# An encoder layer with expert retrieval on one core: a norm's vector moved to the copies, later loads, shares of background work by stage, one value block in three split

## The chip, the cores and the metric

The kernel runs on 1 core of one Trainium2 chip. The time is the device time of one execution in microseconds (us). TensorE (PE) multiplies, with its weight loads (PEld) beside; VectorE (DVE), ScalarE (ACT) and GpSimd (POOL) work on elements; SyncE (SP) issues transfers, as ACT and POOL also do.

## The reference

Two batches of 256 tokens each (prompt and sample), preceded by 16 learned meta tokens, pass one layer of width 1024:

```python
def layer(h, tables, norm_mix_g, w_in, conv_w, ...):
    xn = rmsnorm(h, norm_mix_g)
    z = xn @ w_in
    gate_b, gate_c, hc, q, k, v = jnp.split(z, IN_SPLITS, axis=-1)
    y_conv = group_rmsnorm(gate_b * depthwise_conv3(gate_c * hc, conv_w), conv_out_g, CONV_GROUPS)
    ...
    y_attn = group_rmsnorm(gqa_attention(q, k, v), attn_out_g, N_HEADS)
    h = h + jnp.concatenate([y_conv, y_attn], axis=-1) @ w_out
    h = h + peer_ffn(rmsnorm(h, norm_ffn_g), peer_wq, peer_subkeys, peer_u, peer_v)
    return h

def peer_ffn(x, wq, subkeys, u_tab, v_tab):
    q = (xf @ wq).reshape(T, PEER_HEADS, 2, PEER_HALF)
    s = jnp.einsum('thpc,hpnc->thpn', q, subkeys)
    sv, si = lax.top_k(s, PEER_TOPK)
    ...
    cv, cp = lax.top_k(cand, PEER_TOPK)
    eidx = jnp.take_along_axis(cand_idx, cp, axis=-1)
    gates = jax.nn.softmax(cv, axis=-1)
    uc = jnp.take(u_tab, eidx, axis=0)
    a = jax.nn.gelu(jnp.einsum('thkd,td->thk', uc, xf), approximate=False) * gates
    vc = jnp.take(v_tab, eidx, axis=0)
    return jnp.einsum('thk,thkd->td', a, vc)
```

cand are the 16 x 16 sums of the best scores of two halves, so each token chooses 8 heads x 16 of 16384 experts. All numbers are fp32.

## The kernel before

The experts of the two batches are computed in two ways. For the prompt the rows of the chosen experts are **gathered**: one indirect transfer (grow, 1 MB) brings u and v of one expert for each of 128 tokens; DVE makes a dot product of u and x (a "dot"), ACT the gelu and the gate (dots), DVE adds the weighted v to the output row (xh, a "value"). There are 256 such gathers, in a ring of four buffers. For the sample all 16384 experts are computed **densely**: 128 blocks of u against all tokens (pSj), a dense matrix of gates made on the chip (pgm), and 128 blocks of v against the weighted result A (acc).

PE's stages, in the order of the program:

- *First front end* (s=0, to 135 us): norm, transposes (`norm_T`), input projection, convolution, attention, output projection. Each product is split into three fp32r terms (high and low parts: whi, wlo, xT, lo).
- *First projections* (to 189 us): queries, key scores (`key_scores`), top-k of token tile 0 on DVE.
- *Second front end* (s=1, to 341 us): the same with plain fp32 matmuls. Beside it runs background work: the gathers, and the top-k of tile 1 as a task.
- *Second projections* (to 415 us), with key scores put off by `lag=3`.
- *U stage* (to 924 us): the loop over 128 blocks of u (128x1024, 512 KB each). `experts` applies the gelu to four blocks at a time (SG). The task `gates_dense` ends the top-k (`fin1`), transposes idx_i and idx_j (pi) and the gates (pg), makes one-hot masks oi and oj on DVE and their scaled copies gh and gl on ACT, and multiplies them on PE (pgm), four tokens a step; each pair of steps is then multiplied into A (Al and Ah, blocks 0 to 91 and 92 to 127).
- *Values stage* (to 1345 us): `values(j)` for 128 blocks of v, loaded in pairs. A block is direct (eight fp32 matmuls of 128x512) or, one in SPL, split: ACT makes ah and vh (vhl), DVE al and vl, and PE twelve fp32r matmuls. vhl has one pair of buffers.

The order of the background work is set when the program is written. `bg(us)` follows each piece of PE work and gives credits: `share["a"]` of the microseconds to gathers (each costs GU=2.65), `share["b"]` to tasks, whose `yield` numbers say what a step costs. `gather()` then emits a dot, a value and the next issues. In the values stage the gathers that are left are spread evenly over the blocks. Each engine works through its instructions in that order; POOL issues a gather when a ring buffer is free, and not before the matmul that stood last on PE when it was emitted (`sync_dep`).

SP's queue carries the loads of x, weights, u and v; ACT's queue a few others: gf (the second norm's vector, broadcast to 512 KB) at the start and dc0 (192 KB, constants for decoding the top-k) at the first projections. xg is the first norm's vector, broadcast to 512 KB and used in the norm:

```python
dve.scalar_tensor_tensor(x, h[:, t, :], stat, xg, op0=ALU.mult, op1=ALU.mult)          # 494
act.activation(dst(cs), pt, AF.Copy)                                                   # 466
dve.tensor_tensor(dst_lo(cs), pt, dst(cs).bitcast(F32), op=ALU.subtract)               # 468
```

Of the kernel before, what the change touches and what calls it, by code (L numbers as in the profile page):

```python
# [8 lines left out]
F32 = mybir.dt.float32  # L9
# [3 lines left out]
AF = mybir.ActivationFunctionType  # L13
ALU = mybir.AluOpType
# [4 lines left out]
P = 128  # L19
D = 1024  # L20
NC = 8
NT = 4
SEQ = 256
NM = 16
# [12 lines left out]
JH = 92  # L37
SF = 0.5
SB0 = 0.35
SR = 0.6  # L40
SS = 0.72
SMAX = 0.74
SPL = 4
SBS = 0.42
# [3 lines left out]
def encoder_layer(ctx: ExitStack, tc: tile.TileContext, xp, xs_, meta, vec, w_in, w_out, wq,  # L48
                  skT, qkg, gffn, gmixr, rope, iota16, dec, u_t, uv, v_n, yp, ys):
    nc = tc.nc  # L50
# [326 lines left out]
    def projections(xr, sk, scores, qp, step=None, split=False, rescale=None, lag=1):  # L377
# [3 lines left out]

        def key_scores(hp, qs):
            pn = pst.tile([P, 2, P], F32, tag="tr", name="pn")
            for t in range(2):
                pe.matmul(pn[:, t, :], qs[:, t * P:(t + 1) * P], sk[:, hp, :], start=True, stop=True)
            if hp < 2 and rn is not None:
                for t in range(2):
                    act.activation(scores[:, hp, t], pn[:, t], AF.Copy, scale=rn[:, t:t + 1])
            else:
                act.activation(scores[:, hp], pn, AF.Copy)  # L390
            if step is not None and hp % 2:
                step(hp // 2)

        for hd in range(PH):
            w = weights(wq, hd, split)
            for pp in range(2):
# [9 lines left out]
                bg(3.9)  # L406
        while late:
            key_scores(*late.pop(0))

# [19 lines left out]
    nc.sync.dma_start(vecs, vec)  # L429
    xg = one.tile([P, D], F32, name="xg")  # L430
    nc.sync.dma_start(xg, bass.AP(tensor=gmixr.tensor, offset=gmixr.offset, ap=[[0, P], [1, D]]))
    w_kv = weights(w_in, 0, True)
# [7 lines left out]
    gf = one.tile([P, D], F32, name="gf")  # L440
    act.dma_start(gf, bass.AP(tensor=gffn.tensor, offset=gffn.offset, ap=[[0, P], [1, D]]))

# [16 lines left out]
    def norm_T(dst, x, dst_lo=None):  # L459
        for c4 in range(2):  # L460
            pt = (pst, pss)[c4].tile([P, 4, P], F32, tag=("tr", "sc")[c4], name="pt")
            for cc in range(4):
                c = 4 * c4 + cc
                pe.transpose(pt[:, cc, :], x[:, c * P:(c + 1) * P], ident)
            cs = slice(4 * c4, 4 * c4 + 4)
            act.activation(dst(cs), pt, AF.Copy)
            if dst_lo is not None:
                dve.tensor_tensor(dst_lo(cs), pt, dst(cs).bitcast(F32), op=ALU.subtract)

    def front(s, h, rn):  # L470
# [17 lines left out]
        for t in range(2):  # L488
# [4 lines left out]
            x = tmp.tile([P, D], F32, tag="xs", name="xs")  # L493
            dve.scalar_tensor_tensor(x, h[:, t, :], stat, xg, op0=ALU.mult, op1=ALU.mult)
            tok = slice(NM + t * P, NM + (t + 1) * P)
            norm_T(lambda c: xT[:, c, tok], x, (lambda c: xTl[:, c, tok]) if sp else None)
            bg(1.2)
        if s == 0:
# [3 lines left out]
            rsqrt(mstat[:, 1:2], mstat[:, 0:1], 1, 1.0 / D)  # L502
            dve.scalar_tensor_tensor(mt, mt, mstat[:, 1:2], xg[:NM], op0=ALU.mult, op1=ALU.mult)
            pm = pst.tile([P, NC, NM], F32, tag="tr", name="pm")
            for c in range(NC):
                pe.transpose(pm[:, c, :], mt[:, c * P:(c + 1) * P], ident[:NM, :NM])
            act.activation(xTm, pm, AF.Copy)
        dve.tensor_copy(xT[:, :, 0:NM], xTm)
# [24 lines left out]
        def k_T(a, rows, dst):  # L533
# [5 lines left out]
            act.activation(dst, pk[:, :, :rows], AF.Copy)  # L539

        w = w_kv if s == 0 else weights(w_in, 0)
        for t in (0, 1, -1) if s == 0 else (0, 1):
# [142 lines left out]
        def conv_fin(i, cstat):  # L685
# [9 lines left out]
            if sp:  # L695
                act.activation(catT[:, i, :], yn, AF.Copy)
                dve.tensor_tensor(catTl[:, i, :], yn, catT[:, i, :].bitcast(F32), op=ALU.subtract)

        st = {}
        cs_ = None  # L700
# [23 lines left out]
        def turn(sl):  # L724
# [6 lines left out]
            for c in range(2):  # L731
                k = 2 * sl + c
                act.activation(xr[:, k], pt[:, c], AF.Copy, scale=vecs[:, 8 + k:9 + k])
                if sp:
                    dve.scalar_tensor_tensor(xrl[k // 4][:, k % 4], pt[:, c], vecs[:, 8 + k:9 + k], xr[:, k].bitcast(F32),
                                             op0=ALU.mult, op1=ALU.subtract)

        for sl in range(4):
            w = weights(w_out, sl, sp)
# [42 lines left out]
    dc0 = r0p.tile([P, 3, 16, 16], F16, name="dc0")  # L782
    act.dma_start(dc0, dec)
    sc0 = r0p.tile([P, NC * (LK + 256)], F32, tag="sc", name="sc0")[:, :32 * P].rearrange("p (h t n) -> p h t n", h=16, t=2)
# [26 lines left out]
    queue.extend((0, k) for k in range(P))  # L811
    share.update(a=SF, b=SB0)
    rn1 = selp.tile([P, 2], F32, name="rn1")
# [59 lines left out]
    share.update(a=SR, b=0.0)  # L873
    projections(xr1, sk1, sc1, q1, step1, rescale=rescale, lag=3)
    direct[0] = True
# [7 lines left out]
    def gates_dense():  # L883
# [4 lines left out]
        topk_left[0] = -1  # L888
        yield 10.0
        ogx = ExitStack()  # L890
# [34 lines left out]
        for t in range(2):  # L925
# [12 lines left out]
            for r in range(2):  # L938
                act.activation(dup[:, 0:2, :, r], pi, AF.Copy)
            yield 1.6  # L940
            for o in range(P // OC):
                s0 = o * OC
# [12 lines left out]
                if len(steps) > 1:  # L955
                    gate_products(*steps.pop(0))
                yield 1.3 + (4 * r_done[0] + 60) / 700
        gate_products(*steps.pop(0))
        ogx.close()

    tasks.append(gates_dense())
    share.update(a=SS, b=SBS)
    late = []
# [14 lines left out]
    for j in range(P):  # L978
# [8 lines left out]
        if j % SG == 0 and j:  # L987
            experts(*late.pop(0))
        bg(3.5)
    experts(*late.pop(0))  # L990
# [57 lines left out]
def layout(**inputs):  # L1048
# [15 lines left out]
    def wl(a):  # L1064
# [26 lines left out]
        skT=c(g("peer_subkeys")[0].reshape(16, P, P).transpose(2, 0, 1)),  # L1091
        qkg=qkg, gffn=g("norm_ffn_g"), gmixr=g("norm_mix_g"), rope=rope, iota16=iota, dec=dec,
        u_t=c(u.reshape(P, P, NC, P).transpose(3, 1, 2, 0).reshape(P, P, D)), uv=c(np.concatenate([u, v], axis=1)), v_n=v)
# [19 lines left out]
```

## Time and profile before

| | |
|---|---|
| median of 3 runs | 1352.38 us (1351.4 to 1353.75) |
| profiled execution | 1352.28 us, span 1350.5 us, mean granted clock 0.984 |
| PE busy | 1275.4 us, 94% of the span |
| PEld, DVE, ACT, POOL busy | 957.6, 1043.2, 536.2, 387.4 us |
| bytes moved | 460.19 MB, 341 GB/s over the span |
| chain that ended last | PE 51%, transfers 10%, DVE 8% of the span |

Busy shares are means over stages with different limits. The windows view gives them by stage, the list of waits says what ended PE's idle time, and the timeline shows single instructions with their start and length. A row names the engine, the line, the operation, the tile written and the tiles read.

### The profile page before, as it was taken

The numbers are of one execution on the slowest core, as the hardware profiler recorded it, in microseconds if no ns is written. First come the engines' busy times: TensorE is split into PE (matmuls) and PEld (weight loads), VectorE is DVE, ScalarE is ACT, GpSimd is POOL, SyncE is SP. The second block draws the span as 40 slices with busy tenths as digits, with TensorE's granted clock in tenths as the row PEclk, the third lists the DMA queues.
The fourth block names the chain that finished last, engine by engine and source line by source line (L and its number), as shares of the span: only waits on it lengthen the run. The fifth ranks groups of instructions, "written<-read, shape, count | busy, mean of one in ns | idle before, by whom it ended". The sixth has DMA issues, their size and how long they took to land.

```text
span 1350.5 us, 17724 instructions
## 1 busy us (share of the span) xinstructions
PE 1275.4 (94%) x5998; PEld 957.6 (71%) x5998; DVE 1043.2 (77%) x2247; ACT 536.2 (40%) x1576; POOL 387.4 (29%) x480
## 2 busy tenths in 40 slices
PE   5999998888898999779999999998999999999998
PEld 5888996667787887668788888885555555555554
DVE  5656998976699998688887978986767667676665
ACT  4555531752221311176776766641222222222121
POOL 1111124432242334434332322332222223223121
PEclk9999998998998999979999999999999999999999
DMA  5434646576998999999999999999999999999997
GB/s 204 131 103 159 205 123 228 203 267 255 374 326 293 365 418 416 417 383 413 386 405 387 416 408 400 404 413 421 404 403 396 406 401 405 404 395 408 400 402 283
DMA packets 81003, 460.19 MB, mean 341 GB/s; under 512 B 9473, under 2 KB 9985, under 8 KB 39697
## 3 DMA queue, kind: packets, MB, share of 16 engines
q0 software_dynamic: 37296, 270.02, 49.9%
q1 hardware_dynamic: 41888, 183.37, 36.1%
q10 hardware_dynamic: 1728, 5.67, 1.2%
q8 instruction: 47, 0.77, 0.2%
q14 instruction: 44, 0.35, 0.1%
HBM read 454.81 MB, written 4.19 MB: 340 GB/s over the span
## 4 chain that ended last, share of the span: by engine, by line
PE 51%; DMA 10%; DVE 8%; issue 1%; ACT 1%; POOL 0%; DVEq 0%; POOLq 0%
PE acc L1029 30%; PE pSj L138 19%; DMA grow<-in_uv,eidx 10%; DVE Al L65 2%; DVE xh L65 2%; DVE grow L65 2%; PE pgm L908 1%; PE pgm L909 1%; DVE Ah L65 1%; DVE s L65 0%; POOL cd L294 0%; ACT dots L65 0%; DVE c L65 0%; DVE hd L65 0%; ACT gh L65 0%
## 5 line engine op out<-in xcount | busy, mean ns | idle before, releaser
L180 POOL DMA_INDIRECT grow<-in_uv,eidx x256 | 310.6, 1213 | 733.2 <-PE acc L1029 229.7
L138 PE MATMUL pSj<-xr,u 128*128 128x256 f32 x2048 | 468.7, 386 | 4.6 <-ACT Al L65 2.7
L138 PEld LDWEIGHTS pSj<-xr,u 128*128 128x128 f32 x2048 | 387.5, 193 | 62.8 <-DMA u<-in_u_t 6.4
L65 DVE SCALAR_TENSOR_TENSOR grow<-grow,xh 128x1024 f32<-128x1024 f32 x256 | 312.7, 1221 | 143.3 <-DMA grow<-in_uv,eidx 141.9
L65 DVE SCALAR_TENSOR_TENSOR xh<-grow,dots,xh 128x1024 f32<-128x1024 f32 x256 | 328.1, 1282 | 62.9 <-ACT dots L65 61.8
L65 ACT ACTIVATE dots<-dots 128x1 f32<-128x1 f32 x256 | 51.8, 202 | 525.2 <-DVE grow L65 524.3
L1029 PE MATMUL acc<-v,Al 128*128 128x512 f32 x552 | 240.7, 593 | 0.7 <-DMA v<-in_v_n 0.7
L1029 PEld LDWEIGHTS acc<-v,Al 128*128 128x128 f32 x552 | 104.9, 190 | 123.8 <-issue 120.8
L65 ACT ACTIVATE gh<-oj,ghi 128x128 f16<-128x128 f16 x256 | 99.7, 389 | 8.3 <-PE pgm L908 4.7
L65 ACT ACTIVATE gl<-oj,glo 128x128 f16<-128x128 f16 x256 | 99.7, 389 | 0.0
L1029 PE MATMUL acc<-v,Ah 128*128 128x512 f32 x216 | 94.2, 592 | 0.0
L1029 PE MATMUL acc<-vhl,ah 128*128 128x512 f32 x256 | 81.7, 441 | 2.8 <-ACT vhl L65 2.8
L65 ACT ACTIVATE dots<-dots,gate_all 128x1 f32<-128x1 f32 x256 | 74.7, 292 | 6.8
L1029 PEld LDWEIGHTS acc<-v,Ah 128*128 128x128 f32 x216 | 41.1, 190 | 48.0 <-issue 47.3
L1029 PEld LDWEIGHTS acc<-vhl,ah 128*128 128x128 f32 x256 | 48.1, 188 | 26.1 <-issue 14.8
L65 DVE TENSOR_TENSOR wlo<-w,whi 128x1024 fp32r<-128x1024 f32 x42 | 50.9, 1216 | 18.6 <-PE pc L138 11.3
L138 PE MATMUL pqq<-xr,w 128*128 128x256 f32 x256 | 58.1, 380 | 2.9 <-DMA w<-in_wq 1.8
L65 ACT ACTIVATE vhl<-v 128x1024 fp32r<-128x1024 f32 x32 | 33.8, 1056 | 53.9 <-DMA v<-in_v_n 51.4
L138 PEld LDWEIGHTS pqq<-xr,w 128*128 128x128 f32 x256 | 47.6, 190 | 9.3 <-DMA w<-in_wq 2.2
L65 ACT ACTIVATE whi<-w 128x1024 fp32r<-128x1024 f32 x42 | 43.8, 1054 | 17.0 <-PE pqq L138 9.5
L138 PE MATMUL pc<-xT,w 128*128 128x258 f32 (+1 forms) x192 | 47.4, 398 | 2.9 <-DVE rb L65 2.4
L908 PE MATMUL pgm<-gh,oi 128*128 128x128 f16 x256 | 36.3, 221 | 14.1 <-ACT gh L65 11.4
(278 smaller groups left out, 1724.5 us busy)
## 6 DMA issues: line engine op xcount, KB each, us to landing
u<-in_u_t SPq DMA_DIRECT2D x128, 512.0 KB, 8.5
v<-in_v_n SPq DMA_DIRECT2D x64, 1024.0 KB, 9.1
w<-in_w_in SPq DMA_DIRECT2D x36, 512.0 KB, 4.6
w<-in_wq SPq DMA_DIRECT2D x32, 512.0 KB, 4.7
w<-in_w_out SPq DMA_DIRECT2D x16, 512.0 KB, 4.0
grow<-in_uv,eidx POOLq DMA_INDIRECT x256, 9.7
hdram<-h ACTq DMA_DIRECT2D x3, 512.0 KB, 4.1
h<-in_xp SPq DMA_DIRECT2D x2, 512.0 KB
```

Source lines behind the costliest of these rows:

```text
L65: i = f(*a, **k)
L138: i = pe.matmul(out, st_(c, a), mv(c, b), start=(n == 0), stop=(n == NC * len(terms) - 1))
L180: i = pool.indirect_dma_start(out=r, out_offset=None, in_=uv, in_offset=bass.IndirectOffsetOnAxis(ap=eidx[:, t, k:k + 1], axis=0))
L908: pe.matmul(pg[:, q, :], oi[:, r, :], gh[:, r, :], start=True, stop=False)
L909: pe.matmul(pg[:, q, :], oi[:, r, :], gl[:, r, :], start=False, stop=True)
L1029: i = pe.matmul(acc[t][q], a[:, t * P:(t + 1) * P], v[:, q * 512:(q + 1) * 512], start=j == 0 and n == 0, stop=j == P - 1 and n == len(ter ...
```

## The change

xg, its input and its load are gone. x is scaled by the row statistic alone (on DVE in the first front end, on ACT in the second), and the norm's vector, of which vecs holds a column for each chunk of 128, is applied when the transposed chunks are copied out of PSUM, one chunk at a time. gf and dc0 go through SP's queue, gf behind rp, dc0 behind the weights that are emitted ahead of it. The shares of the second front end are set by stage instead of once. The last three key scores of the second projections are emitted in the first three U blocks; the gates task starts at block 3, with other step costs. SPL is 3: 42 blocks of 128 are split instead of 32.

```diff
-SF = 0.5
-SB0 = 0.35
-SPL = 4
+SPL = 3
...
-        def key_scores(hp, qs):
-            pn = pst.tile([P, 2, P], F32, tag="tr", name="pn")
+        def key_scores(hp, qs, pl=None, tag="tr"):
+            pn = (pl or pst).tile([P, 2, P], F32, tag=tag, name="pn")
...
-        while late:
-            key_scores(*late.pop(0))
+        if lag > 1:
+            return lambda pl, tag: late and key_scores(*late.pop(0), pl, tag)
+        key_scores(*late.pop(0))
...
-    xg = one.tile([P, D], F32, name="xg")
-    nc.sync.dma_start(xg, bass.AP(tensor=gmixr.tensor, offset=gmixr.offset, ap=[[0, P], [1, D]]))
...
-    act.dma_start(gf, bass.AP(tensor=gffn.tensor, offset=gffn.offset, ap=[[0, P], [1, D]]))
+    nc.sync.dma_start(gf, bass.AP(tensor=gffn.tensor, offset=gffn.offset, ap=[[0, P], [1, D]]))
...
-            cs = slice(4 * c4, 4 * c4 + 4)
-            act.activation(dst(cs), pt, AF.Copy)
-            if dst_lo is not None:
-                dve.tensor_tensor(dst_lo(cs), pt, dst(cs).bitcast(F32), op=ALU.subtract)
+            for cc in range(4):
+                c = 4 * c4 + cc
+                act.activation(dst(c), pt[:, cc, :], AF.Copy, scale=vecs[:, c:c + 1])
+                if dst_lo is not None:
+                    dve.scalar_tensor_tensor(dst_lo(c), pt[:, cc, :], vecs[:, c:c + 1], dst(c).bitcast(F32),
+                                             op0=ALU.mult, op1=ALU.subtract)
...
-            dve.scalar_tensor_tensor(x, h[:, t, :], stat, xg, op0=ALU.mult, op1=ALU.mult)
+            if sp:
+                dve.tensor_scalar_mul(x, h[:, t, :], stat)
+            else:
+                act.activation(x, h[:, t, :], AF.Copy, scale=stat)
...
-            dve.scalar_tensor_tensor(mt, mt, mstat[:, 1:2], xg[:NM], op0=ALU.mult, op1=ALU.mult)
+            act.activation(mt, mt, AF.Copy, scale=mstat[:, 1:2])
...
-            act.activation(xTm, pm, AF.Copy)
+            for c in range(NC):
+                act.activation(xTm[:, c], pm[:, c], AF.Copy, scale=vecs[:, c:c + 1])
...
+        if s == 1:
+            share.update(a=0.2, b=0.3)
         w = w_kv if s == 0 else weights(w_in, 0)
...
+        if s == 1:
+            share.update(a=0.45, b=0.35)
         st = {}
...
+        if s == 1:
+            share.update(a=0.7, b=0.3)
         for sl in range(4):
             w = weights(w_out, sl, sp)
...
-    act.dma_start(dc0, dec)
+    nc.sync.dma_start(dc0, dec)
...
-    share.update(a=SF, b=SB0)
+    while len(pend) < len(ring):
+        g_issue()
+    share.update(a=0.2, b=0.3)
     rn1 = selp.tile([P, 2], F32, name="rn1")
     xr1 = front(1, hs1, rn1)
...
-    projections(xr1, sk1, sc1, q1, step1, rescale=rescale, lag=3)
+    rest = projections(xr1, sk1, sc1, q1, step1, rescale=rescale, lag=3)
...
-        yield 10.0
+        yield 6.0
...
             yield 1.6
+            yield 3.0
             for o in range(P // OC):
...
                     gate_products(*steps.pop(0))
+                if o == 0:
+                    yield 2.0
                 yield 1.3 + (4 * r_done[0] + 60) / 700
...
-    tasks.append(gates_dense())
-    share.update(a=SS, b=SBS)
...
+        if j < 3:
+            rest(psg, "g")
+        if j == 3:
+            tasks.append(gates_dense())
+            share.update(a=SS, b=SBS)
         bg(3.5)
```

Where the first gate products stand on PE. In these rows pSj are U blocks of eight matmuls each (x312 is 39 blocks), pi and pg the transposes of indices and gates, pgm the products of a mask (oi) and a scaled mask (gh, gl). Before:

```order
L385 MATMUL pn<-Ah,qs 128x128 x8
L138 MATMUL pSj<-xr,u 128x256 x312
L927 LDWEIGHTS idx_i
L927 MATMUL pi<-ident_5105,idx_i 128x128
L928 LDWEIGHTS idx_j
L928 MATMUL pi<-ident_5105,idx_j 128x128
L930 MATMUL pg<-ident,gate_all 128x128
L138 MATMUL pSj<-xr,u 128x256 x16
L908 LDWEIGHTS oi
L908 MATMUL pgm<-gh,oi 128x128
```

And with the change:

```order
L136 MATMUL pSj<-xr,u 128x256 x16
L383 MATMUL pn<-Ah,qs 128x128
L136 MATMUL pSj<-xr,u 128x256 x8
L383 MATMUL pn<-Ah,qs 128x128 x2
L136 MATMUL pSj<-xr,u 128x256 x304
L938 LDWEIGHTS idx_i
L938 MATMUL pi<-ident_5156,idx_i 128x128
L939 LDWEIGHTS idx_j
L939 MATMUL pi<-ident_5156,idx_j 128x128
L941 MATMUL pg<-ident,gate_all 128x128
L136 MATMUL pSj<-xr,u 128x256 x48
L919 LDWEIGHTS oi
```

Three of the last key-score matmuls (pn) now lie between the first three blocks; 41 blocks (2 + 1 + 38) instead of 39 precede the transposes, and six instead of two lie between them and the first product, whose weights are loaded from oi.

Where the U stage ends on PE, last rows before the first matmul of the values stage (acc). Before, with seven blocks behind the last product:

```order
L908 LDWEIGHTS oi
L908 MATMUL pgm<-gh,oi 128x128
L909 LDWEIGHTS oi
L909 MATMUL pgm<-gl,oi 128x128
L138 MATMUL pSj<-xr,u 128x256 x56
L1029 MATMUL acc_0_8178<-v,Al 128x512
```

And with the change, where the last 24 products follow the last U block:

```order
L920 MATMUL pgm<-gl,oi 128x128
L919 LDWEIGHTS oi
L919 MATMUL pgm<-gh,oi 128x128
L920 LDWEIGHTS oi
L920 MATMUL pgm<-gl,oi 128x128
L1046 MATMUL acc_0_8187<-v,Al 128x512
```

On DVE the same place now reads as follows (xh and grow are a gather's value and dot, Ah<-pSj the product of an expert block with the gates, Al<-pgm and Ah<-pgm the update of A by a pair of product steps):

```order
L63 TENSOR_TENSOR oj<-dup,io 128x512
L63 TENSOR_TENSOR oi<-dup,io 128x512
L63 SCALAR_TENSOR_TENSOR xh<-grow,dots,xh 128x1024
L63 SCALAR_TENSOR_TENSOR grow,dots<-grow,xh 128x1024
L63 SCALAR_TENSOR_TENSOR xh<-grow,dots,xh 128x1024
L63 SCALAR_TENSOR_TENSOR grow,dots<-grow,xh 128x1024
L63 TENSOR_TENSOR Ah<-pSj,Ah 128x4x240
L63 SCALAR_TENSOR_TENSOR Al<-pgm,Al 128x92x8
L63 SCALAR_TENSOR_TENSOR Ah<-pgm,Ah 128x36x8
L63 TENSOR_TENSOR oi<-dup,io 128x512
L63 SCALAR_TENSOR_TENSOR Al<-pgm,Al 128x92x8
L63 SCALAR_TENSOR_TENSOR Ah<-pgm,Ah 128x36x8
```

The last mask oi stands behind two gathers, the last expert block's product and the update of A by the pair of steps before.

## Rows read from the trace of the kernel before

**Rows 1.** Busy us (x instructions) by stage: PE, PEld, DVE, ACT, POOL; PEclk, DMA share, GB/s.

```profile
189.00:341.00 152.00, 131.95 (x642) 104.34 (x641) 122.17 (x414) 65.29 (x164) 53.49 (x101) 0.96 0.63 228
415.50:557.00 141.50, 140.02 (x621) 117.26 (x622) 128.19 (x333) 30.28 (x84) 53.35 (x62) 0.99 0.97 382
924.00:1345.20 421.20, 418.26 (x1152) 218.22 (x1152) 284.75 (x354) 91.75 (x256) 106.09 (x93) 1.00 0.98 396
```

**Rows 2.** The same view, pieces of the second front end and of the values stage.

```profile
189.00:310.00 121.00, 101.48 (x499) 79.09 (x498) 104.38 (x381) 56.22 (x129) 45.56 (x95) 0.95 0.61 217
920.00:960.00 40.00, 36.57 (x105) 19.38 (x104) 27.87 (x34) 9.44 (x26) 9.14 (x9) 1.00 1.01 419
1000.00:1040.00 40.00, 40.00 (x112) 20.83 (x111) 26.82 (x35) 8.56 (x24) 11.32 (x10) 1.00 0.99 400
```

**Rows 3.** What PE waited for in the second projections: total, times, longest us.

```profile
PE pn L385 <- ACT Ah L65: 3.5, 1, 3.5
```

**Rows 4.** What PE waited for from 416 to 600 us.

```profile
PE pgm L908 <- ACT gh L65: 11.4, 1, 11.4
PE pSj L138 <- ACT Al L65: 2.7, 1, 2.7
```

**Rows 5.** What PE waited for from 600 us to the end.

```profile
PE acc L1029 <- ACT vhl L65: 2.8, 1, 2.8
```

**Rows 6.** Timeline of the start: start us, us, engine, line, operation.

```profile
12.01 1.28 DVE L65 SCALAR_TENSOR_TENSOR xs<-h,stat,xg 128x1024 f32<-128x1024 f32 x1
...
13.34 1.97 PE L464 MATMUL pt<-ident,xs 128*128 128x128 f32 x8 [13.34 <-DVE xs L65]
...
14.49 0.60 ACT L65 ACTIVATE xT<-pt 128x512 fp32r<-128x512 f32 x1 [0.46 <-PE pt L464]
...
15.12 0.69 DVE L65 TENSOR_TENSOR lo<-pt,xT 128x512 fp32r<-128x512 f32 x1 [0.64 <-ACT xT L65]
```

**Rows 7.** Groups of instructions by line and shape, first front end: xcount, busy us, mean ns.

```profile
L65 ACT ACTIVATE catT<-pty,vecs 128x128 fp32r<-128x128 f32 x8 | 2.9, 358 | 1.5 <-PE pty L635 1.0 <-DVE lo L65 0.4
L65 DVE SCALAR_TENSOR_TENSOR lo<-pty,vecs,catT 128x128 fp32r<-128x128 f32 x8 | 2.8, 346 | 0.1
```

**Rows 8.** Timeline where the gate products begin.

```profile
557.85 0.22 PE L927 MATMUL pi<-ident,idx_i 128*128 128x128 f16 x1
...
558.40 1.91 POOL L180 DMA_INDIRECT grow<-in_uv,eidx  x1 [1.84 <-PE pg L930]
...
562.15 1.92 POOL L180 DMA_INDIRECT grow<-in_uv,eidx  x1 [1.84 <-DMA grow<-in_uv,eidx]
...
574.54 0.43 ACT L65 ACTIVATE dup<-pi 128x256 f16<-128x256 f16 x1
```

**Rows 9.** Timeline of DVE before the end of the U stage.

```profile
899.20 1.18 DVE L65 TENSOR_TENSOR Ah<-pSj,Ah 128x992 f32<-128x992 f32 x1
...
900.30 0.91 DVE L65 SCALAR_TENSOR_TENSOR Al<-pgm,Al 128x736 f32<-128x736 f32 x1
...
901.43 1.27 DVE L65 SCALAR_TENSOR_TENSOR xh<-grow,dots,xh 128x1024 f32<-128x1024 f32 x1
...
902.62 1.22 DVE L65 SCALAR_TENSOR_TENSOR grow<-grow,xh 128x1024 f32<-128x1024 f32 x1
```

**Rows 10.** Timeline of one period of the values stage.

```profile
1005.67 10.46 PE L1029 MATMUL acc<-v,Al 128*128 128x512 f32 x24
...
1008.90 1.06 ACT L65 ACTIVATE vhl<-v 128x1024 fp32r<-128x1024 f32 x1 [0.76 <-DMA v<-in_v_n]
...
1010.83 0.19 PEld L1029 LDWEIGHTS acc<-v,Al 128*128 128x128 f32 x1 [0.24 <-issue]
...
1012.48 1.22 DVE L65 TENSOR_TENSOR vhl<-v,vhl 128x1024 fp32r<-128x1024 f32 x1
...
1013.61 0.42 DVE L65 TENSOR_TENSOR al<-Al,ah 128x256 fp32r<-128x256 f32 x1
...
1018.73 0.59 PE L1029 MATMUL acc<-v,Al 128*128 128x512 f32 x1
```

More of the change, by code (lines that the diff above doesn't have):

```diff
@@ L48, in encoder_layer @@
 def encoder_layer(ctx: ExitStack, tc: tile.TileContext, xp, xs_, meta, vec, w_in, w_out, wq,
-                  skT, qkg, gffn, gmixr, rope, iota16, dec, u_t, uv, v_n, yp, ys):
+                  skT, qkg, gffn, rope, iota16, dec, u_t, uv, v_n, yp, ys):
     nc = tc.nc
@@ L1091, in layout @@
         skT=c(g("peer_subkeys")[0].reshape(16, P, P).transpose(2, 0, 1)),
-        qkg=qkg, gffn=g("norm_ffn_g"), gmixr=g("norm_mix_g"), rope=rope, iota16=iota, dec=dec,
+        qkg=qkg, gffn=g("norm_ffn_g"), rope=rope, iota16=iota, dec=dec,
         u_t=c(u.reshape(P, P, NC, P).transpose(3, 1, 2, 0).reshape(P, P, D)), uv=c(np.concatenate([u, v], axis=1)), v_n=v)
```

## The prediction

> **What bounds the kernel now.** The profiled execution took 1352.28 us (span 1350.5 us), the median of the runs is 1352.38 us: the sum below is made against 1352.3. I read the busy times by stage first. The reader is to see two kinds of stage in them. In the second front end (189 to 341 us) PE is busy 131.95 of 152.00 us, so 20 us are lost there; in the U stage (415.5 to 557) and the values stage PE is busy all but 1.5 and 3 us, while the transfers already move 382 and 396 GB/s [rows 1]. Then the same view in shorter pieces: in 189 to 310 us DVE is busy 104.38 of 121.00 us, 86%, and the transfers reach 400 GB/s in an ordinary piece of the values stage and 419 in the busiest one [rows 2]. Last the list of what PE waited for: 3.5 us for a key-score table at the end of the second projections [rows 3], 11.4 and 2.7 us where the gate products begin [rows 4], 2.8 us for the first split value block [rows 5]. So the kernel is bound by PE, except in the second front end and at these joints, where PE waits for a DVE/ACT stream that also carries the gathers.
>
> **Start.** The 512 KB of xg no longer stand ahead of the first weights on SP's queue, and gf and dc0 (704 KB together) no longer run beside them. At the 419 GB/s of [rows 2] that is an estimate of 1.3 to 3 us by which the first weights land earlier; the first transposes waited for xs, which on DVE stood behind a weight's low part [rows 6]. gf is first used at the end of this front end and dc0 at the end of the projections behind it, over 100 us later, so four weights put ahead of dc0 cost nothing; without that cover it would be their own transfer. Against it stand the copies: for each tile ACT makes eight of 128x128 (0.36 each, 2.9 us) for two of 0.60 (1.2), DVE eight of 0.35 (2.8) for two of 0.69 (1.4) [rows 6, 7]. Most lies under PE's own three matmuls for each chunk, and PE can begin after one chunk, not four. Bounds: -3 (all the transfer time) to +2 (the added DVE and ACT time of the first tile, nothing earlier). I take **-1**, since xs and not the weight was what PE waited for. The plain scaling by stat of 128x1024 on DVE has no row; its nearest is the xs row (1.28), and that is its upper bound. The Trainium skill ("VectorE: DVE Perf Modes", "The perf-mode tier table") lets an fp32 operation with one tensor source in SBUF run at twice the rate; by that it would be an estimate of 0.64 us, and the start 0.6 us earlier still.
>
> **Second front end.** The order of DVE shows 29 gather operations (dots and value updates) ahead of the first output projection before and 21 now, since the share falls from 0.5 to 0.2 and rises only at the convolution. Eight operations at 1.22 to 1.28 [rows 9] are 10.0 us. Two norms of 1.28 [rows 6] leave DVE for ACT: 2.6. With 86% of the stretch filled by DVE [rows 2] I count 12.6 x 0.86 = 10.8. ACT's smaller copies add 2 x 1.7 = 3.4 on the path from the norm to the first matmul. That gives **-7**; bounds -12.6 (DVE sets every wait) and +3.4 (PE's 20 us are latencies of chains that no gather stands in, and only the copies count). The top-k tasks of the other tile keep a share of about 0.3 and stay in front of the same place. The four gathers that the new loop issues ahead change nothing: in POOL's order the first four stand where they stood.
>
> **End of the projections and start of the gates.** The last three key scores move behind the first U blocks, so the 3.5 us of [rows 3] go; but what PE waited for there was the stream, and the stream is late next at the gates. PE had the index transposes at 557.85 us, and ACT copied them out at 574.54: 16.7 us behind [rows 8]. In the changed order 41 U blocks instead of 39 stand ahead of them and six instead of two behind, before the first product. The third product group's operands stand on ACT behind seven more gathers, because the buffers oi and gh are two deep. POOL issues gathers every 3.75 us there [rows 8], and eight U blocks take 8 x 3.59 = 28.7 us (140.02 / 39 in [rows 1]). The stream would then be ready 16.7 + 3.5 - 3.75 (one gather fewer is ahead by then) + 7 x 3.75 = 42.7 us after the transposes, and PE would wait 14.0 us in all, against 11.4 + 2.7 + 3.5 = 17.6 now [rows 3, 4]. I take **-3**. Bounds: -17.6 if DVE catches up, +4 if nine gathers rather than seven come in between.
>
> **End of the U stage.** Starting the gates 2 blocks later, and the longer steps, leave three product groups (24 products) behind the last U block, where before seven blocks lay behind the last group. What PE must wait out is the last expert block's product on DVE (1.18), the update of Al behind the group before (0.91) and the next pair of masks (about 0.4 each, nearest the al row) [rows 9, 10], the eight scaled copies on ACT (nearest 0.36 each, in part beside the products) [rows 7] and again the 0.91: 1.0 + 1.2 + 0.9 + 0.8 + 2.9 + 0.9 = 7.7 us, and up to two gathers (2 x 2.5) if they stand in the way. The 2.8 us in front of the first split block [rows 5] fall under this wait. So **+6**, from +2 (DVE well ahead) to +10.
>
> **Values stage.** A direct block is eight matmuls, one every 0.43 us (0.19 + 0.24): 3.44 us. The period of three direct blocks and one split is 1018.73 - 1005.67 = 13.06 us, so a split costs 2.74 [rows 10]. Ten more of the 128 blocks are split: 10 x 0.70 = -7. But more must be moved in less time: the order leaves 99 gathers, not 94, for this stage, and with 64 v loads of 1 MB that is 163 x 1.05 = 171 MB. In 414 us that needs 413 GB/s, between the 400 and the 419 of [rows 2]. At 419 the full 7 us come; at 400 the stage takes 427 us, +6. I take **-3**, the nearer end being 419, which this very stage shows at its start. The rule against it: the Trainium skill ("DMA: Bandwidth & Descriptors", "Where 436 GB/s comes from") says that about 358 GB/s of memory bind transfers from it and gives 435 for the fabric. The trace disagrees with the first (396 as the mean of a stage that waits for nothing); by it the stage would be an estimate of 477 us, by the second the full 7 us would come.
>
> Sum: -1 - 7 - 3 + 6 - 3 = -8, so **1344 us**.
>
> **Rivals.** *The stream bounds everything behind the front end.* For it: 382 to 419 GB/s from the U stage on, and the change moves no gather byte out of the program, only later. Then the -7 come back as two gathers that are late at the front's end and three at the values, 5 x 1.05 MB / 0.4 = 13 us of transfer, of which the stages' slack takes half: 1352.3 - 1 - 7 + 6 = about 1350 to 1353. Against it: in the values stage PE lost only 3 us in 421.
>
> *The splits wait.* With two direct blocks between splits instead of three, the single pair of buffers vhl comes free 3.44 us later relative to its next use. In the row of before, the preparation ended, with al on DVE, 1013.61 + 0.42 - 1005.67 = 8.4 us after the previous split's end, the low part of v behind a gather's dot [rows 10]; two direct blocks and the first third of the split, which al is not needed for, give 6.9 + 0.9 = 7.8 us. Each of 42 splits that waits d costs 42 d: the term turns to a loss from d = 0.17 us, the whole change from d = 0.36. At d = 0.5 it is +21 instead of the reserve of 4: 1352.3 - 1 - 7 - 3 + 6 + 14 = **1361 us**, slower. Against it: some of the 8.4 us is DVE waiting for a dot's rows, and these operations stand one block earlier in the new order.
>
> *The gate joint closes wholly* and the end of U is covered: 1352.3 - 1 - 7 - 17.6 + 2 - 5 = **1324 us**, or 1332 if it closes by half. For it: the added yields put the products later than PE needs; against it the third group's two-deep buffers.
>
> **How the numbers follow.** Forecast 0.50, stream 0.18, splits wait 0.20, joint closes 0.12. A measurement can tell 0.2%, 2.7 us. Faster: 0.47 of the forecast's cases, 0.12 and 0.03 of the stream's = 0.62. Slower: 0.20 and 0.01 = 0.21. Same: 0.17. The forecast's own terms reach from about 1335 to 1352; the range takes in half of the closing joint and splits that wait 0.4 us: 1331 to 1358.
>
> **What would show it.** Right: PE idle in the second front end near 13 us, not 20; a PE wait of about 14 us at the third product group; a wait of 4 to 9 us between the last U block and the first value block; a period of two direct blocks and a split near 9.6 us with transfers at 410 GB/s or more. Wrong: waits in front of most split blocks, transfers that stay at 400 while v loads come late, or a front end as long as before.

## The result and the profile after

The median is **1346.09 us** (1342.24 to 1348.04, 8 runs) against 1353.75 us (1351.4 to 1357.86, 8 runs) on the same chip: a ratio of 0.9927, 95% interval 0.9907 to 0.9948. The prediction was 8 us less; measured are 7.7. The profiled execution took 1346.99 us, its span is 1345.2 us.

Stage by stage, from the first instruction of each stage on PE (transposes, queries, first U block, first value block) to the last value block, one profiled execution each:

| us | PE starts | first front end | first projections | second front end | second projections | U stage | values stage | rest of the span |
|---|---|---|---|---|---|---|---|---|
| before | 13.3 | 122.0 | 53.9 | 151.4 | 74.9 | 508.6 | 421.0 | 5.3 |
| changed | 12.7 | 121.0 | 53.9 | 146.6 | 74.4 | 517.7 | 414.8 | 4.1 |
| changed, again | 11.5 | 123.7 | 53.9 | 139.5 | 76.8 | 514.9 | 414.5 | 4.1 |

So in these executions time is won in the second front end (5 to 12 us) and in the values stage (6), and the U stage gives back 6 to 9. What of this is the change's doing, the experiments tell. The busy times by stage of the changed kernel (us, then PE, PEld, DVE, ACT, POOL, PEclk, DMA share, GB/s), to be read beside [rows 1]:

```profile
187.60:334.20 146.60, 133.19 (x638) 104.54 (x636) 118.14 (x401) 61.64 (x168) 47.91 (x97) 0.95 0.61 220
914.00:926.30 12.30, 1.77 (x22) 1.36 (x19) 7.23 (x12) 4.52 (x15) 2.36 (x2) 0.62 0.93 353
926.30:1341.10 414.80, 414.14 (x1192) 225.81 (x1192) 306.10 (x384) 103.55 (x281) 112.07 (x96) 0.99 0.98 406
```

PE idles 13.4 us in the second front end, not 20. The middle row is new: in 12.3 us between the U blocks and the values PE works 1.8, at a mean granted clock of 0.62 of full speed, a mixture of its two levels (1.2 and 2.4 GHz). In the values stage PE idles 0.7 us, at 406 GB/s on average. In shorter pieces, beside [rows 2]:

```profile
187.60:307.00 119.40, 109.46 (x538) 84.64 (x536) 99.64 (x373) 53.57 (x136) 43.13 (x92) 0.97 0.57 200
307.00:334.20 27.20, 23.73 (x100) 19.91 (x100) 18.49 (x29) 8.07 (x32) 4.78 (x5) 0.87 0.82 307
1000.00:1040.00 40.00, 40.00 (x117) 21.80 (x116) 29.15 (x39) 10.00 (x28) 11.43 (x10) 1.00 1.01 421
```

DVE is busy 99.6 of 119.4 us in the first piece, 83%, where it was 86%. In the second, PE's granted clock is 0.87 after several short waits. An ordinary piece of the values stage now moves 421 GB/s, where it moved 400.

What PE waited for in the whole program, to be read beside [rows 3 to 5]:

```profile
PE pgm L919 <- DVE oi L63: 15.1, 2, 9.6
PE pt L461 <- DVE ss L63: 12.7, 1, 12.7
PE acc L1046 <- DMA v<-in_v_n: 5.1, 1, 5.1
PE pSj L136 <- ACT Ah L63: 4.7, 1, 4.7
PE pb L877 <- ACT dg L63: 3.5, 1, 3.5
...
PE acc L1046 <- DVE al L63: 0.6, 1, 0.6
```

pn, the wait of [rows 3], is gone, and 4.7 us stand at the first U block instead (pSj). The first row holds two waits for a mask, 9.6 us at the gate joint and 5.5 at the end of the U stage. The v load's 5.1 us are the other part of that end. (pt is the start; pb, the row factors in the second projections, waits 3.5 us for ACT.) No split block waited more than 0.6 us for its parts.

The start, beside [rows 6]:

```profile
10.70 1.23 DVE L63 TENSOR_TENSOR wlo<-w,whi 128x1024 fp32r<-128x1024 f32 x1
...
11.85 0.75 DVE L63 TENSOR_SCALAR xs<-h,stat 128x1024 f32<-128x1024 f32 x1
...
12.65 1.97 PE L461 MATMUL pt<-ident,xs 128*128 128x128 f32 x8 [12.65 <-DVE ss L63]
...
13.80 0.37 ACT L63 ACTIVATE xT<-pt,vecs 128x128 fp32r<-128x128 f32 x1 [0.54 <-PE pt L461]
...
14.21 0.35 DVE L63 SCALAR_TENSOR_TENSOR lo<-pt,vecs,xT 128x128 fp32r<-128x128 f32 x1 [0.41 <-ACT xT L63]
```

The scaling by stat alone takes 0.75 us, not 1.28. By the Trainium skill ("VectorE: DVE Perf Modes", "The perf-mode tier table") an fp32 operation with one tensor source in SBUF runs at twice the rate, and 0.64 us was the estimate from it; the trace gives 0.11 more. The copies take the 0.37 and 0.35 of [rows 7]. In DVE's order xs now stands behind the low parts of two weights (the second is the wlo row), where before it stood behind one. The gate joint, at the third product group, beside [rows 8]:

```profile
559.41 0.22 PE L938 MATMUL pi<-ident,idx_i 128*128 128x128 f16 x1
...
588.73 3.72 PE L136 MATMUL pSj<-xr,u 128*128 128x256 f32 x16 [0.50 <-ACT Al L63]
...
598.52 1.23 DVE L63 SCALAR_TENSOR_TENSOR grow<-grow,xh 128x1024 f32<-128x1024 f32 x1 [0.50 <-DMA grow<-in_uv,eidx]
...
600.35 1.28 DVE L63 SCALAR_TENSOR_TENSOR xh<-grow,dots,xh 128x1024 f32<-128x1024 f32 x1 [0.60 <-ACT dots L63]
...
601.55 0.42 DVE L63 TENSOR_TENSOR oi<-dup,io 128x512 f16<-128x512 f16 x1
...
602.03 0.29 PE L919 MATMUL pgm<-gh,oi 128*128 128x128 f16 x1 [9.58 <-DVE oi L63]
```

PE stood from 592.4 (the end of the pSj row) to 602.0 us while DVE worked through gathers ahead of the mask oi. The mask was ready at 601.97 us, 42.6 after the transposes began (pi). The end of the U stage:

```profile
917.43 1.15 DVE L63 TENSOR_TENSOR Ah<-pSj,Ah 128x960 f32<-128x960 f32 x1
...
918.50 0.92 DVE L63 SCALAR_TENSOR_TENSOR Al<-pgm,Al 128x736 f32<-128x736 f32 x1
...
919.70 0.42 DVE L63 TENSOR_TENSOR oi<-dup,io 128x512 f16<-128x512 f16 x1
...
920.17 0.29 PE L919 MATMUL pgm<-gh,oi 128*128 128x128 f16 x1 [5.47 <-DVE oi L63]
...
921.27 1.80 SPq L1026 DMA_DIRECT2D v<-in_v_n  x3
...
926.26 6.29 PE L1046 MATMUL acc<-v,Al 128*128 128x512 f32 x9 [5.05 <-DMA v<-in_v_n]
```

DVE's order is that of the prediction: the expert block's product, the update of Al, oi, then PE's last products. What the prediction did not have is the row of SP's queue. The first v load is issued at 921.27 us, right behind the last product, and PE waits for it until 926.26. These waits cost more than their length, as the granted clock (0.50, the third number from the end) shows:

```profile
925.00:930.00 5.00, 3.74 (x5) 1.71 (x6) 0.28 (x1) 1.06 (x1) 0.00 (x0) 0.50 1.02 429
```

PE had been nearly idle from 914 us, and from 920 to 930 the clock was at its lower level. So the first nine matmuls of the values stage took the 6.29 us of the row above, where sixteen take 7.03 later (967.02 below): the first value block is 2.3 us longer than the others, and 2.6 us in the second execution. And a period of the values stage, beside [rows 10]:

```profile
967.02 7.03 PE L1046 MATMUL acc<-v,Al 128*128 128x512 f32 x16
...
969.80 1.06 ACT L63 ACTIVATE vhl<-v 128x1024 fp32r<-128x1024 f32 x1 [0.98 <-DMA v<-in_v_n]
...
972.64 0.42 DVE L63 TENSOR_TENSOR al<-Al,ah 128x256 fp32r<-128x256 f32 x1
...
973.49 1.48 PE L1046 MATMUL acc<-vhl,ah 128*128 128x512 f32 x4
...
976.64 7.03 PE L1046 MATMUL acc<-v,Al 128*128 128x512 f32 x16
```

From 967.02 to 976.64 us are 9.62 us for two direct blocks and a split, which is 2 x 3.44 + 2.74 to the hundredth.

### The profile page after: what moved, and what is told of

It reads as the page before. It is cut to its first block, busy times and chain, and to the rows that moved or that the text cites. A ratio compares the mean times of both kernels' runs of the same rounds, so it can differ in the third digit from the quotient of the medians.

```text
span 1345.2 us, 17868 instructions
## 1 busy us (share of the span) xinstructions
PE 1275.6 (95%) x6038; PEld 965.0 (72%) x6038; DVE 1056.0 (78%) x2279; ACT 549.9 (41%) x1621; POOL 389.1 (29%) x480
## 4 chain that ended last, share of the span: by engine, by line
PE 37%; DMA 17%; DVE 7%; issue 3%; ACT 2%; POOL 0%; DVEq 0%; POOLq 0%; ACTq 0%; SPq 0%
PE acc L1046 27%; DMA grow<-in_uv,eidx 16%; PE pSj L136 9%; DVE xh L63 3%; DVE grow L63 2%; DMA v<-in_v_n 1%; DVE Ah L63 1%; ACT dots L63 1%; DVE Al L63 1%; PE pgm L920 1%; PE pgm L919 1%; ACT gh L63 0%; ACT pSj L63 0%; DVE vhl L63 0%; ACT gl L63 0%
## 5 line engine op out<-in xcount | busy, mean ns | idle before, releaser
L178 POOL DMA_INDIRECT grow<-in_uv,eidx x256 | 317.2, 1239 | 717.2 <-DVE xh L63 233.5
L1046 PE MATMUL acc<-v,Al 128*128 128x512 f32 x496 | 220.1, 597 | 5.1 <-DMA v<-in_v_n 5.1
L1046 PEld LDWEIGHTS acc<-v,Al 128*128 128x128 f32 x496 | 94.9, 191 | 113.0 <-issue 110.5
L1046 PE MATMUL acc<-vhl,ah 128*128 128x512 f32 x336 | 107.4, 441 | 0.0
L63 DVE TENSOR_TENSOR vhl<-v,vhl 128x1024 fp32r<-128x1024 f32 x42 | 51.4, 1224 | 55.6 <-ACT vhl L63 55.6
L1046 PEld LDWEIGHTS acc<-vhl,ah 128*128 128x128 f32 x336 | 63.2, 188 | 30.2 <-issue 19.1
L1046 PE MATMUL acc<-v,Ah 128*128 128x512 f32 x192 | 84.3, 592 | 0.0
L63 DVE TENSOR_TENSOR wlo<-w,whi 128x1024 fp32r<-128x1024 f32 x42 | 51.1, 1218 | 19.6 <-ACT whi L63 13.4
L1046 PEld LDWEIGHTS acc<-v,Ah 128*128 128x128 f32 x192 | 36.4, 190 | 41.2 <-issue 40.2
L919 PE MATMUL pgm<-gh,oi 128*128 128x128 f16 x256 | 36.8, 222 | 16.1 <-DVE oi L63 15.1
L63 ACT ACTIVATE vhl<-v 128x1024 fp32r<-128x1024 f32 x42 | 44.0, 1048 | 19.1 <-DMA v<-in_v_n 18.4
```

The source lines that it names most:

```text
L63: i = f(*a, **k)
L178: i = pool.indirect_dma_start(out=r, out_offset=None, in_=uv, in_offset=bass.IndirectOffsetOnAxis(ap=eidx[:, t, k:k + 1], axis=0))
L919: pe.matmul(pg[:, q, :], oi[:, r, :], gh[:, r, :], start=True, stop=False)
L1046: i = pe.matmul(acc[t][q], a[:, t * P:(t + 1) * P], v[:, q * 512:(q + 1) * 512], start=j == 0 and n == 0, stop=j == P - 1 and n == len(ter ...
```

## The experiments

Each ran several times beside the kernel before: a0 and e1 to e3 on one chip, e4 to e7 on a second, e8 to e10 on a third, e11 on a fourth. The stages of all, from one profiled execution each (e1, e2, e4 to e7 and e10 start from the changed kernel, e8, e9 and e11 from e5, e3 from the kernel before):

| us | second front end | second projections | U stage | values stage | median | ratio to before, interval |
|---|---|---|---|---|---|---|
| changed, again (a0) | 139.5 | 76.8 | 514.9 | 414.5 | 1341.69 | 0.991 (0.9881 to 0.9939) |
| e1, cheaper steps | 143.0 | 78.2 | 512.8 | 417.4 | 1343.36 | 0.9908 (0.9879 to 0.9936) |
| e2, SPL 4 | 141.1 | 77.5 | 516.6 | 420.6 | 1352.71 | 0.9982 (0.9962 to 1.0002) |
| e3, before with SPL 3 | 152.7 | 73.4 | 507.8 | 414.9 | 1345.03 | 0.9932 (0.9907 to 0.9956) |
| e4, old shares | 149.0 | 71.9 | 515.0 | 414.4 | 1340.11 | 0.99 (0.987 to 0.993) |
| e5, old step costs | 146.1 | 76.9 | 506.5 | 416.6 | 1341.03 | 0.9912 (0.9878 to 0.9946) |
| e6, old joint | 144.8 | 79.7 | 515.0 | 413.1 | 1345.12 | 0.9943 (0.9921 to 0.9964) |
| e7, old norm | 140.5 | 77.7 | 517.6 | 414.9 | 1339.68 | 0.9914 (0.9883 to 0.9945) |
| e8, pace 0.55 / 0.84 | 149.3 | 77.7 | 512.2 | 414.0 | 1344.18 | 0.9894 (0.9859 to 0.9928) |
| e9, SPL 2 | 142.5 | 77.2 | 504.6 | 417.4 | 1340.3 | 0.9891 (0.9863 to 0.9919) |
| e10, 16 gathers fewer | 141.9 | 77.6 | 514.7 | 412.7 | 1343.41 | 0.9909 (0.9881 to 0.9936) |
| e11, pace 0.60 / 0.78 | 141.7 | 77.0 | 505.1 | 415.5 | 1333.54 | 0.9848 (0.9829 to 0.9866) |

The first thing to learn from it is the spread: the second front end of a0, e1, e2 and e5 to e11 has the same shares as the changed kernel's 146.6 us, and it took 139.5 to 149.3. A difference of 5 us in that stage between two single executions says nothing.

**a0: the changed kernel again.**

> The changed kernel again, beside the three that follow. Both theories: 1346 us, ratio 0.993 to the kernel before; the wait of about 10 us between the U stage and the values stage is there again (5.5 for the last mask oi, 5.1 for the first v load), as is that of about 10 us at the third product group.

1341.69 us. Both waits were there: 5.4 and 5.05 us at the end, 9.4 at the third group. The list of waits of SP's queue (what it waited for, us, times, longest) from 880 to 945 us names what held the first v load:

```profile
SPq L1026 <- PE pgm L920: 22.3, 1, 22.3
```

**e2 and e3: SPL alone, both ways.**

```diff
-SPL = 3
+SPL = 4
```

> Of the changed kernel SPL is put back to 4. Theory: ten more direct blocks of 3.44 us for splits of 2.74, 7 us: 1353 us, period of four blocks 13.06 us, transfers at 405 GB/s in the values stage. Rival (the stream): the values stage is set by its bytes, 1346 us.

> Of the kernel before SPL alone is changed to 3. Theory: -7 us in the values stage (period of three blocks 9.62 us), 1346 to 1347 us against 1353. Rival (splits wait where the v loads and DVE are less well ahead): waits of 0.2 us and more at each split, 1350 or more.

e2 lies within the noise of the kernel before (0.9982), e3 near the changed one (0.9932). The values stage of e2, then that of e3:

```profile
922.00:1342.60 420.60, 420.58 (x1152) 218.90 (x1152) 289.45 (x360) 91.11 (x259) 118.94 (x96) 0.99 0.97 400
```

```profile
923.60:1338.50 414.90, 413.03 (x1192) 226.30 (x1192) 299.13 (x375) 102.36 (x276) 111.27 (x93) 1.00 0.99 403
```

6.1 us shorter with SPL 3 each time (420.6 to 414.5, and 421.0 to 414.9), and the rest of the span behind the last value block 1.2 to 1.4 us shorter: the last block, 127, is direct with SPL 3, so its four accumulators end one after the other and DVE's four additions begin earlier. Nearly all that the change gains is this one constant.

**e4: the old shares in the second front end.**

```diff
-        if s == 1:
-            share.update(a=0.2, b=0.3)
...
-    share.update(a=0.2, b=0.3)
+    share.update(a=0.5, b=0.35)
     rn1 = selp.tile([P, 2], F32, name="rn1")
```

> Of the changed kernel the shares in the second front end are put back (0.5 and 0.35 throughout); the norm, the four early issues, the joint and SPL stay. Theory: eight more gather operations on DVE ahead of the output projection, so the second front end takes 4 to 7 us longer, and half of it comes back later, since two gathers fewer are left: 1345 to 1349 us. Rival (the norm's move alone shortened the front end): stage as in the changed kernel, 146 us, 1343 us.

The stage took 149.0 us, at the upper edge of the spread of the others and inside it, with 29 gather operations on DVE ahead of the first output-projection result instead of 22. But the whole was 1340.11 us, no slower. The second projections took 71.9 us instead of some 77, and the waits from 330 to 925 us moved:

```profile
PE acc L1040 <- DMA v<-in_v_n: 10.4, 1, 10.4
PE pSj L136 <- ACT Al L63: 9.0, 3, 3.7
...
PE pgm L913 <- ACT gh L63: 1.5, 1, 1.5
```

PE lost 1.5 + 9.0 us in four waits around the gate joint, and 10.4 at the end of the U stage, and the U stage took what it took in a0 (515.0 and 514.9). The second front end and the second projections together took 220.9 us; in the runs with the new shares they took 216.3 to 227.0. So what the shares give in the front end, as far as one execution tells, is given back by the end of the second projections; the theory's "half" was too little.

**e7: the old norm.**

```diff
-                act.activation(dst(c), pt[:, cc, :], AF.Copy, scale=vecs[:, c:c + 1])
+            act.activation(dst(cs), pt, AF.Copy)
...
+            dve.scalar_tensor_tensor(x, h[:, t, :], stat, xg, op0=ALU.mult, op1=ALU.mult)
```

> Of the changed kernel the norm is put back (xg loaded and multiplied on DVE, copies of four chunks); the rest stays. Theory: the first transposes start at 13 us instead of 12, and the first front end ends 1 to 2 us later; the second loses another 1: 1344 to 1346 us. Rival (xs was not what bound the start): no change, 1343 us.

PE started at 12.0 us, the first front end took 122.4, the second 140.5, and the median is 1339.68 us: no loss that can be told, so the norm's move gave nothing that these runs can show. e7 still starts 1.4 us earlier than the kernel before; what is left to explain it is the loads that were put later, which no run put back alone.

**e1: the gates end earlier.**

```diff
-                yield 1.3 + (4 * r_done[0] + 60) / 700
+                yield 1.1 + (4 * r_done[0] + 60) / 700
```

> Of the changed kernel one number is changed: a product step of the gates task costs 1.1 + ... instead of 1.3 + ..., so the 64 steps are emitted closer together and six U blocks lie behind the last product instead of none. Theory: the first v loads wait for the last product (the buffers of the gates task must be given back), and that wait and the one for oi, 10.5 us together, go; 1337 us, PE waits under 2 us between the stages. Rival (the stream of transfers is the bound): what PE no longer waits there it waits later, in the values stage, whose period then grows over 9.62 us; 1344 to 1346.

1343.36 us, no faster than the changed kernel beside it. The mechanism showed: the v load's wait fell to 0.7 us and oi's at the end went. But the first joint's wait stayed (9.7 us), and waits at the second token tile's are new (3.4 of the first row, and pg):

```profile
PE pgm L919 <- DVE oi L63: 13.1, 2, 9.7
...
PE pg L941 <- ACT dup L63: 2.4, 1, 2.4
...
PE acc L1046 <- DMA v<-in_v_n: 0.7, 1, 0.7
```

The U stage shrank by 2 us instead of 9, and the values stage took 417.4 us, 2.9 more than in a0, so a part came back there, as the rival had it.

**e5: the old step costs, and e6: the whole old joint.**

```diff
-        yield 6.0
+        yield 10.0
...
-            yield 3.0
...
-                if o == 0:
-                    yield 2.0
```

> Of the changed kernel the step costs of the gates task are put back (10.0, no 3.0, no 2.0), so two U blocks, not six, lie between the transposes and the first product; the task still starts at block 3, and one U block, not none, lies behind the last product. Theory: the wait at the gate joint grows back to some 14 us, at the first product; the end of the U stage still waits some 5 to 10 us: 1347 us. Rival: the stream's lag alone counts, where the products stand does not; 1343 us.

> Of the changed kernel the whole joint is put back: key scores in the projections, gates task from block 0, old step costs. Norm, loads, shares and SPL stay. Theory: pn waits 3.5 us again and the first U block no longer 5; 14 us at the first product; none at the end of the U stage (five blocks behind the last product): sum of these about 18 us against 27 in the changed kernel, so faster than it, 1336 to 1340 us. Rival (the joint's rearrangement is worth what it was made for): 1346 or more.

e5's 14.5 us stand at the first product, as expected, and the end costs 1.6, not 5 to 10, so its U stage is 8 us shorter than a0's (e9, the same up to there, took 504.6):

```profile
PE pgm L919 <- ACT gh L63: 14.5, 1, 14.5
...
PE acc L1043 <- DVE Al L63: 1.6, 1, 1.6
```

Its median, 1341.03 us, lies beside a0's, so a gain of the whole isn't shown, and where the 8 us went stays open. e6 brings back the pn wait and takes the 5 us at the first U block away:

```profile
PE pgm L918 <- ACT gh L63: 18.7, 3, 12.8
...
PE pn L383 <- ACT Ah L63: 4.7, 2, 3.7
...
PE pSj L136 <- ACT Ah L63: 0.5, 1, 0.5
```

1345.12 us: not the gain that was expected from summing waits; 18.7 us of gh in three waits ate it. e5 and e6 differ in where the key scores and the start of the task stand. Against the changed kernel's two ratios (0.9927 and 0.991) that of e6, 0.9943, is 2 to 5 us slower, and the intervals overlap: that the rearranged joint gains anything isn't shown.

**e8 and e11: fewer gathers ahead of the joint, more behind.** From e5:

```diff
-            share.update(a=SS, b=SBS)
+            share.update(a=0.55, b=SBS)
...
+                if t == 0 and o == 2:
+                    share.update(a=0.84)
                 steps.append((t * P + s0, oi, gh, gl))
```

> The kernel of e5 with the gathers' share set in two parts: 0.55 from block 3 to the third product step, 0.84 behind it, so 70 dots instead of 77 stand on DVE ahead of the third step's mask, and 97 gathers are left for the values stage instead of 100. Theory: the wait at the joint (16 us in e5) is DVE's lag behind gathers whose rows come every 3.75 us; seven fewer take it to under 5, and the transfers fit later, where the U stage moves 390 GB/s: 10 us faster than e5, some 1331. Rival (the stream of transfers bounds everything from the second projections on): the waits come back behind the joint, 1340.

The wait at the first joint went wholly (16 us to 0). In its place the second token tile's joint and a later mask waited, and the first v load 4.1 us:

```profile
PE pgm L919 <- DVE oi L63: 11.1, 3, 8.2
...
PE pg L941 <- ACT dup L63: 4.1, 1, 4.1
```

The median is 1344.18 us, not 1331: the rival, that the waits come back behind the joint, has it.

e11 takes 0.60 and 0.78:

> A middle between e5 and e8: share 0.60 from block 3 to the third product step, 0.78 behind it (98 gathers left for the values stage). Theory: DVE's lag at the first joint falls by some five gathers, and DVE behind it is loaded less than in e8, so the wait at the first joint is 4 to 8 us and those at the second token tile stay under 5: 1333 to 1337. Rival (a gather taken from ahead of a joint costs as much wait behind it): 1340 as e5.

**1333.54 us** (1331.91 to 1333.8), ratio 0.9848: faster than the kernel before by 1.5% and clear of the changed kernel, whose interval begins at 0.9881. The first joint again waits for nothing; its list, without one wait of 0.3 us:

```profile
PE pgm L919 <- DVE oi L63: 6.9, 2, 5.3
PE pSj L136 <- ACT Ah L63: 5.2, 1, 5.2
PE acc L1045 <- DMA v<-in_v_n: 3.8, 1, 3.8
PE pg L941 <- ACT dup L63: 3.4, 1, 3.4
```

The size came out as expected, the place did not: in the profiled executions its U stage is only 1.4 us shorter than e5's, and the two differ by 4.5 us (1338.31 and 1333.8), of which the second front end, alike in both kernels and spread over 10 us, could account for 4.4. So that e11 is faster is shown, and that the joint makes it so is not; why its runs lie so close together stays open too.

**e9: every second block split.** From e5, `SPL = 2`:

> The kernel of e5 with SPL = 2: 64 blocks split instead of 42. Theory: a period of two blocks would be 3.44 + 2.74 = 6.2 us and the stage 396, but its 172 MB need 408 us at the 421 GB/s that the changed kernel shows, and one direct block between splits leaves vhl free for 3.4 us only, which its 1.1 + 1.2 + 0.4 us of preparation do not fit behind a gather: waits at many splits, 410 to 420 us, no faster than e5 (1339 to 1346). Rival (PE's matmuls alone count): 14 us faster than e5.

1340.3 us, and the values stage 417.4 instead of e5's 416.6. PE idled 9.3 us in it, half of that at the first split and the rest in many waits of at most 0.6 us, most of them for the split's parts:

```profile
PE acc L1043 <- ACT vhl L63: 4.7, 1, 4.7
PE acc L1043 <- ACT ah L63: 2.7, 7, 0.5
```

Here splits do wait, as in the rival of the prediction. That the single vhl comes free too late isn't shown as the cause: the transfers ran at 416 to 421 GB/s in five pieces of 40 us, where a0's best piece has 422, so they may bound this stage as well.

**e10: sixteen gathers left out.** The prompt's output lacks those experts.

```diff
-    queue.extend((0, k) for k in range(P))
+    queue.extend((0, k) for k in range(P) if not 8 <= k < 24)
```

> The changed kernel without 16 of the 256 gathers (entries 8 to 23 of the first token tile: their experts are left out of the prompt's output). Measures who bounds. If PE does, with waits on the stream at three places only: the waits at the first U block and at the joint shrink or go (5 + 12 us), nothing else, 1325 to 1335. If the stream of transfers bounds all from the second projections on: 16 x 1.05 MB at 0.42 MB/us are 40 us, 1305.

1343.41 us: no gain, against both theories. Since credits set the pace, the same number of gathers stands ahead of each joint, and the waits stay (6.4, 9.4 and 4.7 us); the sixteen are missing at the end. The values stage of e10, then of a0:

```profile
921.20:1334.00 412.80, 412.75 (x1192) 225.92 (x1192) 267.41 (x336) 96.31 (x249) 96.65 (x80) 1.00 0.94 367
```

```profile
920.30:1334.80 414.50, 414.39 (x1192) 226.00 (x1192) 306.57 (x384) 103.04 (x281) 113.87 (x96) 0.99 0.98 406
```

48 DVE instructions and 39 GB/s fewer, and 1.7 us. So the values stage of the changed kernel is not bound by its transfers, at 406 GB/s on average and 422 in the best piece. Of the stages ahead of it e10 says nothing, since there it moves the same bytes.

## Why the prediction was right, and where it was right by chance

- **Start, -1:** PE began 0.7 and 1.8 us earlier in two executions; the first front end ended 1.7 and 0.2 us earlier. Right in size. What the sum did not have is that xs now waits for a second weight's low part, so that an earlier first weight alone does not start PE. The price of the smaller copies, the upper bound's +2, did not show in e7.
- **Second front end, -7:** -4.8 and -11.9. Right in size, within a spread of 10 us. The reason given first (fewer gather operations on DVE) fits best: the three executions with the old shares (before, e3, e4) took 149.0 to 152.7 us, the eleven with the new ones 139.5 to 149.3, and e7, with the old norm, 140.5. What failed is that the step ended there. The prediction had "the stream is late next at the gates" for the 3.5 us of pn, but not for the gathers moved out of the front end. e4, whose whole time is no longer than the changed kernel's, has it given back by the end of the second projections. The rival of the stream described this. Whether its cause, the bytes, is the right one stays open: e10 excludes it for the values stage alone, and around the gate joint (559.4 to 600 us) the changed kernel moved 417 GB/s.
- **End of the projections and gates, -3:** the stall stands at the third group, as worked out, but it was 9.6 + 0.7, not 14.0 us. The stream was priced well, 42.7 us after the transposes against 42.6 and 43.3 measured; PE's work up to there was not, 33.0 us and not 28.7: the sum counted the eight U blocks and left out the two product groups and PE's short waits between them. And the wait for pn was not handed on to the gates: it became 4.7 to 5.9 us at the very next place, the first U block, which waits for ACT's copy of the key scores (by the program, its PSUM is taken from the pool that closes there). Together with the short waits for Al and gl these are 16.1 and 17.9 us against 17.6 before: between -2 and 0.
- **End of the U stage, +6:** the waits were 10.5 us in both executions, 0.7 before. The chain on DVE was right (5.5 us). The step that failed is "what PE must wait out", which looked at PE, DVE and ACT and not at SP: the v loads stood behind the last product, 22.3 us on SP's queue in a0, and then their own 5 us. The step also put the lower clock at nothing, which took 2.3 and 2.6 us in the first value block. Less the 2.8 us of the first split, which did fall under this wait, and the 0.7 of before, the end costs some 9.5 us more. (The prediction's 7.7 has a term, its first 1.0, that no row shows; the five that it names are 6.7, where DVE's part alone measured 5.5.)
- **Values stage, -3:** the stage was 6.2 and 6.5 us shorter, and the tail another 1.2: the full 7 us. e2 against a0, both with the slow first block, gives the same 6.1 and 1.2. The term was mis-sized by the limit put on the transfers, between 400 and 419 GB/s. The 400 of [rows 2] was demand, not capacity: the changed kernel moves 421 when asked, and the page of the kernel before has 416 to 418 GB/s in three slices of 34 us from 473 us on. As for the Trainium skill's two figures ("DMA: Bandwidth & Descriptors", "Where 436 GB/s comes from"): 421 GB/s over 40 us contradicts the 358 for this single core and agrees with the 435 as a ceiling. Splits did not wait: al was ready 972.64 + 0.42 - 967.02 = 6.0 us after the split, not 8.4, which fits the rival's counter-argument, that DVE's work stands a block earlier. (That rival turns the whole change to a loss from d = 12 / 42 = 0.29 us a split, not 0.36.)

The sum came out by luck, since two errors cancel: the second projections and the U stage took 8.6 and 8.2 us more where +3 was forecast, and the values stage with the tail gave 7.4 and 7.7 where 3 was forecast. By e2 and e3 the short account is: SPL alone gives what the whole change gives (0.9932 against 0.9927), and everything else together is worth 0 to 0.4% (e2's interval, 0.9962 to 1.0002), 0 to 5 us. The forecast had it the other way round, -5 for everything else and -3 for SPL.

## What to carry to other kernels

Where in-order queues share one stream of background work, a wait that is taken away can come back at the next place that depends on the stream, as in e1, e4 and e8: price the next place too, and ask how much of the stream stands ahead of it. A transfer rate that a stage shows while nothing waits is its demand, and no capacity. When a wait is added at a stage's end, list who gives back the buffers that the next stage's loads need (the load's own queue is the one that is easily forgotten), and add what the lower clock takes behind the wait.

## What was not expected of the hardware

One stage can differ between executions by as much as the whole (spans of 1345.2 and 1338.9 us): the second front end took 146.6 and 139.5 us in two executions of the changed kernel, and 139.5 to 149.3 in nine executions of kernels that are alike there (without e7 and e10). The transfers hold 415 to 422 GB/s through the values stage (ten slices of 34 us on the page of the changed kernel), where the page of the kernel before has 395 to 408 behind the first 21 us of that stage. And the granted clock, 0.62 as a mean of the 12 us between the U stage and the values, in which PE was busy for 1.8, was still 0.50 in the first 4 us of the values.
